# Gate weight sums beside branch B, and the gate products without sums first

## The chip, the cores and the metric

The kernel runs on one core of a Trainium2 chip. The metric is device time in microseconds. The core has five engines with a queue of instructions each: TensorE (PE, matrix products), VectorE (DVE), ScalarE (ACT), GpSimd (POOL) and SyncE (SP), which here issues every DMA. Each queue is worked off in its own order; an instruction that waits for a semaphore holds back all that stand behind it on its queue.

## The reference, cut to what matters

One encoder block: two attention branches, merged by gates, then a feed-forward part. The gates are what the change is about.

```
h = concat([meta, x])                                # 16 + 1024 tokens, width 1024
proj = rms_norm(h, norm_mix) @ w_in                  # qa ka va | qb kb vb | ga gb
y_a = differential_attention(qa, ka, va, ...)        # branch A: 4 heads, two softmaxes each
y_b = windowed_gqa(qb, kb, vb, sink)                 # branch B: 8 heads, a window of 128
merged = sigmoid(ga) * (y_a @ w_ba) + sigmoid(gb) * (y_b @ w_bb)
h = h + merged @ w_o
h = h + (silu(n @ w_ff_gate) * (n @ w_ff_up)) @ w_ff_down      # n = rms_norm(h, norm_ffn)
out = rms_norm(h, norm_final)[:, 16:]
```

## The kernel before, in words

All matrix products run on operands split in a high and a low part (three matmuls: high by high, high by low, low by high). The normalized tokens lie transposed in SBUF as `hT_hi` and `hT_lo`, and the projections (`project`, line 204 issues their matmuls) run over them, one block of 128 columns of `w_in` after another; each block's weights are loaded to `w_c`, split by ACT (`wh_c`) and POOL (`wl_c`), with two buffers each. In the names, c1280 is the block va2, c768 is ka2, c384 is qa3.

The gate projections (`ga`, `gb`: 16 blocks of 128 columns, 1024 tokens) are computed by a scheme of the Strassen kind: for each of eight chunks `k` of 256 columns seven half-size products `p` (numbered 1 to 7) take the place of eight. Products 2 and 1 use plain weights and plain tokens. Product 3 uses a sum of weights with plain tokens, product 4 plain weights with a sum of tokens, products 5, 6 and 7 sums of both. So two sets of sums are made ahead:

- the token sums (`token_sums`, lines 512 to 529, POOL adds, buffers `ta` and `to` in the pool `tpool`), stored to DRAM as `ts_d` beside branch B's first unit, and brought back later over the part of `hT` that is no longer needed (`load_sums`, line 568);
- the weight sums (`weight_sums`, lines 585 to 597): for each chunk two loads `gw`, four POOL adds (lines 592 to 595) and four stores to `ws_d`. They use a pool of their own, `wspool`.

Order of the stages: normalization and the first projections; unit 0 of branch B (`units_b`, eight score tiles of four heads) mixed with the projections of branch A's heads 0 and 1; the projection qb of unit 1, whose stores `qb` place it for the scores; unit 1 mixed with the projections of heads 2 and 3; then branch A, 32 tiles (head `h`, tile `t` of 128 tokens). In branch B a tile's scores (`bps`) go through DVE and ACT to `bs`, POOL scales them (line 330), PE transposes (`bpt`) and multiplies with the values (`bpy`), and the result goes out as `yb_d`. In branch A a tile's two score rows (`aps`, line 745) go through DVE (line 748), ACT's exponential (line 753), POOL's scaling of the first (line 756) and DVE's combination (line 759), and are transposed (`apt`, line 771) and multiplied with the values (`apy`, line 784).

The gate products fill PE in branch A. `gate_steps` (line 718) is a generator: one step is three matmuls, a product is four steps, and `order_g` lists the 56 products. `fill(n)` takes n steps from it: at the head of branch A (`G_FIRST`), at each later head (`G_HEAD`, 10), and at each "g" of `SLOTS` (5 a tile, 24 tiles) and `SLOTS_LAST` (4 a tile, nine rounds). `HOLD` keeps 36 of the 224 steps for the end. Weights come ahead: `g_load` (line 608; plain ones from `w_in`, sums from `ws_d`, to buffers `gr`) and `g_split` (ACT and POOL, line 118, to `gop`).

In this stage PE's order is the order of the code. On the other engines, and for PE before it, a scheduler sets the order of the whole program from its own estimate of times; once set, it is fixed.

Of the kernel before, what the change touches and what calls it, by code (L numbers as in the profile page):

```python
# [19 lines left out]
P = 128  # L20
# [24 lines left out]
GK_BUFS = 3  # L45
GR_BUFS = 6
GO_BUFS = 4
# [3 lines left out]
G_HEAD = 10  # L51
G_FIRST = 4

# [20 lines left out]
def encoder_block(ctx: ExitStack, tc: tile.TileContext, x, meta, norm_mix, w_in, lq1, lk1, lq2, lk2,  # L74
# [7 lines left out]
    def f32(ap):  # L82
        return ap.bitcast(F32)
# [497 lines left out]
    def g_weights(k, kh, c0, cn):  # L581
        at = (C_GB, C_GA)[k // 4] + k % 4 * 256 + c0
        return w_in[kh * 512:kh * 512 + 512, at:at + cn].rearrange("(c p) n -> p c n", p=P)

    def weight_sums(k, p):
        tt = nc.gpsimd.tensor_tensor
        raw = p.tile([P, 2, 4, 256], F32, tag="raw", name=f"gw_{k}", bufs=2)
        for kh in range(2):
            nc.sync.dma_start(raw[:, kh], g_weights(k, kh, 0, 256))
        a11, a21, a12, a22 = (raw[:, i, :, j * P:j * P + P] for i in range(2) for j in range(2))  # L590
        s1, s2, s3, s4 = (p.tile([P, 4, P], F32, tag="sum", name=f"gs{i}_{k}", bufs=6) for i in range(4))
        tt(s1, a21, a22, ALU.add)
        tt(s2, s1, a11, ALU.subtract)
        tt(s4, a12, s2, ALU.subtract)
        tt(s3, a11, a21, ALU.subtract)
        for i, t in ((5, s1), (3, s4), (6, s2), (7, s3)):
            nc.sync.dma_start(ws_d[i, k], t)

# [37 lines left out]
    qb = new_qb(1)  # L636
    project_qb(1, qb)
    units_b(1, qb)
    close_bpool()
# [11 lines left out]

    def load_a(h):
        p = apool
        qs, ks = [None, None], [None, None]
        for m in (1, 0):
            q = qs[m] = p.tile([P, S], F32R, tag=f"q{m}", name=f"aq{h}_{m}")
            k = ks[m] = p.tile([P, 2, L], F32R, tag=f"k{m}", name=f"ak{h}_{m}")
            nc.sync.dma_start(f32(q), qa_d[h][m])
            nc.sync.dma_start(f32(k)[:, 0, :], ka_d[h][m])
            for hl in range(2):  # L660
                nc.sync.dma_start(f32(k)[64 - 64 * hl:128 - 64 * hl, 1, :], ka_d[h][m, 64 * hl:64 * hl + 64, :])
        v = p.tile([P, 2, 9, P], F32R, tag="v", name=f"av{h}")
        nc.gpsimd.memset(f32(v)[:, 0, 8, :], 0.0)
# [4 lines left out]

    ld = load_a(0)
    wspool, close_wspool = pool("wspool")  # L670
    project_a(2)
    for k in range(4):
        weight_sums(k, wspool)
    project_a(3)
    for k in range(4, 8):
        weight_sums(k, wspool)
    for n in range(2):
        g_load(n, wpool.tile([P, DC, P], F32, tag="w", name=f"w_g{n}", bufs=2)[:, 0:4].rearrange("p c n -> p (c n)"))
        g_split(n, wpool.tile([P, DC, P], F32R, tag=("wh", "wl")[n], name=f"w_gop{n}", bufs=W_BUFS)
                .rearrange("p (a c) n -> p a c n", a=2))  # L680
    g_done[:] = [2, 2]
    load_sums(5, 0, 1)
    flush_v()
    close_psum1()
    close_wspool()
    close_tpool()
# [22 lines left out]
    def gate_steps():  # L709
        for n, (p, k) in enumerate(order_g):  # L710
# [5 lines left out]
            for c in range(4):  # L716
# [3 lines left out]
                if c == 3:  # L720
# [6 lines left out]
                    nc.sync.dma_start(g_place(p, k), st)  # L727
                    if k == 7 and p in (2, 5, 3):
                        load_sums({2: 6, 5: 7, 3: 4}[p], *act)
                yield  # L730
# [720 lines left out]
```

## Time and profile before

| | us |
|---|---|
| median of 3 runs | 1525.5 (1518.1 to 1526.4) |
| the profiled execution | 1522.9 |
| its span | 1521.1 |
| PE, DVE, ACT, POOL busy | 1433.7, 888.8, 679.3, 663.1 |
| end of the projections | 306.8 |
| branch A, first gate step to the last tile's transposes | 306.8 to 655.9 |

The profile is of one execution. Its slices show each engine's busy tenths in 40 equal parts of the span (38 us each) and the clock that TensorE was granted. The list of waits names what ended each idle time. Of the timeline each row is start, duration, engine, line and operands, and in brackets the idle time before it. A row "SPq" is the issue of a DMA, not its transfer. In tables by stretch the columns are named in their first line; where one tile is asked for, they are its engine's busy time and count, the granted clock, the DMA share and GB/s of the stretch.

### The profile page before, as it was taken

The page shows a single profiled execution, that of the slowest core. Times are in us where ns is not written, and L with a number is a line of the kernel's source. Part 1 is how long each engine was busy: PE and PEld are TensorE (multiplying, and loading weights), DVE is VectorE, ACT ScalarE, POOL GpSimd, SP SyncE. Part 2 cuts the span into 40 slices and gives each one's busy share as a digit, 9 for nine tenths or more (in the row PEclk, how much of TensorE's full clock was granted, in tenths as well). Part 3 has the DMA queues.
Part 4 walks back from the last instruction along what each step waited for, and adds up shares of the span by engine and source line. Part 5 has one row for each costly group of instructions (what it writes and reads, how often), then busy time and mean ns, then how long its engine had stood idle before and what let it go on. Part 6 is the DMA issues. An engine that isn't in the chain of part 4 may idle for free.

```text
span 1521.1 us, 21195 instructions
## 1 busy us (share of the span) xinstructions
PE 1433.7 (94%) x7279; PEld 1227.9 (81%) x7279; DVE 888.8 (58%) x1610; ACT 679.3 (45%) x1293; POOL 663.1 (44%) x590
## 2 busy tenths in 40 slices
PE   9999999941699999999999999999999999999997
PEld 7998989931699899987878878888888888788886
DVE  7478336501668687944341596655555554778666
ACT  6466346501466555545431454333333333344444
POOL 4599134328444344333562267545445543000344
PEclk9999999965799999999999999999999999999999
DMA  8457443399364857439650253433333333764443
GB/s 235 110 187 229 115 111 91 89 305 362 119 196 173 282 177 231 131 111 311 192 211 21 97 146 125 139 104 104 104 104 104 104 105 104 282 239 125 137 125 139
DMA packets 185339, 242.41 MB, mean 159 GB/s; under 512 B 18752, under 2 KB 108288, under 8 KB 185232
## 3 DMA queue, kind: packets, MB, share of 16 engines
q1 hardware_dynamic: 185232, 241.07, 49.3%
q8 instruction: 57, 0.93, 0.3%
q14 instruction: 50, 0.41, 0.1%
HBM read 157.45 MB, written 77.00 MB: 154 GB/s over the span
## 4 chain that ended last, share of the span: by engine, by line
PE 72%; DMA 8%; POOL 8%; issue 5%; DVE 3%; ACT 2%; SPq 0%; POOLq 0%; DVEq 0%; ACTq 0%
PE pg L1232 25%; PE pd L1326 8%; PE pg L718 7%; PE po L1009 5%; PE ppa L706 4%; PE aps L745 3%; PE pp_qb L204 3%; PE apy L784 3%; POOL oa L118 3%; PE pp_va L204 2%; PE apt L771 2%; DMA gw<-in_w_in_dram 2%; PE pp_qa L204 2%; PE pp_ka L204 2%; DMA ak<-ka_d 1%
## 5 line engine op out<-in xcount | busy, mean ns | idle before, releaser
L118 POOL TENSOR_TENSOR wop<-wf,wop 128x512 fp32r<-128x512 f32 x128 | 173.3, 1358 | 163.7 <-ACT wop L117 151.4
L1232 PE MATMUL pg<-t,wop 128*128 128x512 f32 x1056 | 242.9, 389 | 0.2 <-POOL wop L118 0.2
L1232 PEld LDWEIGHTS pg<-t,wop 128*128 128x128 f32 x1056 | 198.2, 188 | 41.6 <-POOL wop L118 0.6
L1326 PE MATMUL pd<-ob,oa 128*128 128x512 f32 x924 | 210.2, 390 | 1.3 <-DVE ob L118 0.9
L1326 PEld LDWEIGHTS pd<-ob,oa 128*128 128x128 f32 x924 | 173.4, 188 | 38.0 <-DVE ob L118 1.3
L1232 PE MATMUL pg<-b,wop 128*128 128x512 f32 x792 | 184.0, 390 | 2.3 <-DVE c L1241 2.3
L1232 PEld LDWEIGHTS pg<-b,wop 128*128 128x128 f32 x792 | 148.4, 188 | 33.7 <-issue 2.4
L718 PE MATMUL pg<-hT_hi,gop 128*128 128x512 f32 x432 | 162.7, 399 | 9.9 <-ACT gop L117 7.7
L118 POOL TENSOR_TENSOR gop<-gr,gop 128x512 fp32r<-128x512 f32 x54 | 74.5, 1380 | 121.2 <-ACT gop L117 115.3
L118 POOL TENSOR_TENSOR oa<-ra,oa 128x512 fp32r<-128x512 f32 x33 | 44.0, 1335 | 171.3 <-ACT oa L117 169.9
L117 ACT ACTIVATE wop<-wf 128x512 fp32r<-128x512 f32 x128 | 80.3, 632 | 85.0 <-PE pg L1232 49.3
L745 PE MATMUL aps<-ak,aq 128*128 128x392 f32 (+1 forms) x384 | 96.2, 335 | 13.9 <-DMA ak<-ka_d 13.9
L753 ACT ACTIVATE as<-as,amn 128x1040 f32<-128x1040 f32 x64 | 74.4, 1162 | 76.8 <-DVE amn L748 76.6
L718 PEld LDWEIGHTS pg<-hT_hi,gop 128*128 128x128 f32 x432 | 82.3, 190 | 22.8 <-ACT gop L117 8.0
L117 ACT ACTIVATE oa<-ra 128x512 fp32r<-128x512 f32 x77 | 48.7, 632 | 108.2 <-PE pd L1326 53.2
L745 PEld LDWEIGHTS aps<-ak,aq 128*128 128x128 f32 x384 | 72.1, 195 | 29.9 <-issue 13.8
L1009 PE MATMUL po<-woh,mT 128*128 128x512 f32 x384 | 88.0, 390 | 0.0
L771 PE MATMUL apt<-ident,as 128*128 128x128 f32 x288 | 45.3, 279 | 43.7 <-DVE as L759 43.4
L718 PE MATMUL pg<-hT_lo,gop 128*128 128x512 f32 x216 | 86.1, 398 | 0.0
L1009 PEld LDWEIGHTS po<-woh,mT 128*128 128x128 f32 x384 | 71.9, 188 | 14.8
L1067 DVE TENSOR_TENSOR s<-wf,wf 128x512 f32<-128x512 f32 x22 | 18.8, 856 | 106.6 <-DMA wf<-in_w_ff_gate_dram 55.0
L771 PEld LDWEIGHTS apt<-ident,as 128*128 128x128 f32 x288 | 34.3, 145 | 44.5 <-DVE as L759 43.8
(279 smaller groups left out, 3091.0 us busy)
## 6 DMA issues: line engine op xcount, KB each, us to landing
ra<-aop SPq DMA_DIRECT2D x77, 256.0 KB, 2.7
wf<-in_w_ff_gate_dram SPq DMA_DIRECT2D x24, 512.0 KB, 3.7
wf<-in_w_ff_up_dram SPq DMA_DIRECT2D x24, 512.0 KB, 3.6
aop<-as SPq DMA_DIRECT2D x44, 256.0 KB, 2.1
w_c<-in_w_in_dram SPq DMA_DIRECT2D x17, 512.0 KB, 5.0
aop<-c SPq DMA_DIRECT2D x33, 256.0 KB, 2.0
ts_d<-to SPq DMA_DIRECT2D x16, 512.0 KB, 3.8
gw<-in_w_in_dram SPq DMA_DIRECT2D x16, 512.0 KB, 6.9
```

What stands on the lines that cost most here:

```text
L117: nc.scalar.activation(hi, src, AF.Copy)
L118: lo_eng.tensor_tensor(lo, src, f32(hi), ALU.subtract)
L204: nc.tensor.matmul(ps[:, :n], a[:, c, :], b[:, c, at:at + n], start=(c == 0 and i == 0), stop=(c == DC - 1 and i == 2))
L706: nc.tensor.matmul(ps, w[:, a, j, :], src(j, b, tk), start=(j == 0 and n == 0), stop=(j == 3 and n == 2))
L718: nc.tensor.matmul(ps, op[:, a, c], quad(b, *act)[:, c], start=(p in (2, 5, 1) and c == 0 and i == 0), stop=(p in (2, 3, 4) and c == 3 and ...
L745: nc.tensor.matmul(ps[:, :n], qs[m][:, t * P:(t + 1) * P], ks[m][:, vv, k0:k0 + n], start=(vv == 0), stop=(vv == 1))
L753: nc.scalar.activation(s[m][:, 0:L], s[m][:, 0:L], AF.Exp, bias=low, scale=-1.0, accum_out=dn[:, m:m + 1])
L771: nc.tensor.transpose(pt[:kp, j, :], s[:, k * P:k * P + kp], ident)
L784: nc.tensor.matmul(py[:, cols], v[:kp, a, k, :], at_[:kp, k, b, :], start=(k == 0 and j == 0), stop=(k == 8))
L1009: nc.tensor.matmul(ps, mT[:, c, a, t * P:(t + 1) * P], wos[q, c][:, b], start=(c == 0 and n == 0), stop=(c == DC - 1 and n == 2))
L1232: nc.tensor.matmul(ps, op[:, x, c, :], b[:, y, c, :], start=(p in (1, 2, 5) and c == 0 and n == 0), stop=(p in (4, 2, 3) and c == 3 and n ...
L1326: nc.tensor.matmul(ps[u], oa[:, a, u * P:(u + 1) * P], ob[:, b, :], start=(p in (1, 2, 5) and j == 0 and k == 0), stop=(p in (2, 3, 4) and ...
```

## The change

- The weight sums are made between the projection of qb's unit 1 and that unit's tiles, in halves: a chunk's rows in two pieces `c` of 0 and 2, each with two loads of half the size, four adds of 128x256 for 128x512 and four stores of half the size. They use `tpool`'s buffers, two `to` and three `ta` for all, where `wspool` had two and six.
- `order_g` begins with all eight products 2 (0 to 7); then 5 and 3 in turn; the rest is as before. `G_FIRST` is 28 in place of 4, so that seven products run ahead of branch A's first scores.
- The first two products' weights lie in `tpool`'s buffers in place of `wpool`'s; `GR_BUFS` is 5 in place of 6. The token sums are brought back after (5,3), (5,7) and (3,7), and the first of them between the two parts of head 0's loads, which are now called for after the projections.

```diff
-GR_BUFS = 6
+GR_BUFS = 5
...
-G_FIRST = 4
+G_FIRST = 28
...
-    order_g = [(2, k) for k in range(4)]
+    order_g = [(2, k) for k in range(8)]
     for k in range(0, 8, 2):
         order_g += [(p, k + i) for p in (5, 3) for i in range(2)]
-        if k < 4:
-            order_g += [(2, k + 4 + i) for i in range(2)]
...
-    def weight_sums(k, p):
+    def weight_sums(k):
         tt = nc.gpsimd.tensor_tensor
-        raw = p.tile([P, 2, 4, 256], F32, tag="raw", name=f"gw_{k}", bufs=2)
-        for kh in range(2):
-            nc.sync.dma_start(raw[:, kh], g_weights(k, kh, 0, 256))
-        a11, a21, a12, a22 = (raw[:, i, :, j * P:j * P + P] for i in range(2) for j in range(2))
-        s1, s2, s3, s4 = (p.tile([P, 4, P], F32, tag="sum", name=f"gs{i}_{k}", bufs=6) for i in range(4))
...
+        for c in range(0, 4, 2):
+            raw = tpool.tile([P, 2, 2, 256], F32, tag="to", name=f"gw_{k}_{c}", bufs=2)
+            for kh in range(2):
+                nc.sync.dma_start(raw[:, kh], g_weights(k, kh, 0, 256)[:, c:c + 2])
+            a11, a21, a12, a22 = (raw[:, i, :, j * P:j * P + P] for i in range(2) for j in range(2))
+            s1, s2, s3, s4 = (x[:, i] for x in [tpool.tile([P, 2, 2, P], F32, tag="ta", name=f"gs{j}_{k}_{c}", bufs=3)
+                                                for j in range(2)] for i in range(2))
+            tt(s1, a21, a22, ALU.add)
+            tt(s3, a11, a21, ALU.subtract)
+            tt(s2, s1, a11, ALU.subtract)
+            tt(s4, a12, s2, ALU.subtract)
+            for i, t in ((5, s1), (7, s3), (6, s2), (3, s4)):
+                nc.sync.dma_start(ws_d[i, k][:, c:c + 2], t)
...
     project_qb(1, qb)
+    for k in range(8):
+        weight_sums(k)
     units_b(1, qb)
...
-    ld = load_a(0)
-    wspool, close_wspool = pool("wspool")
     project_a(2)
-    for k in range(4):
-        weight_sums(k, wspool)
     project_a(3)
-    for k in range(4, 8):
-        weight_sums(k, wspool)
     for n in range(2):
-        g_load(n, wpool.tile([P, DC, P], F32, tag="w", name=f"w_g{n}", bufs=2)[:, 0:4].rearrange("p c n -> p (c n)"))
...
+        g_load(n, tpool.tile([P, 512], F32, tag="ta", name=f"w_g{n}", bufs=3))
+        g_split(n, tpool.tile([P, 2, 4, P], F32R, tag="to", name=f"w_gop{n}", bufs=2))
     g_done[:] = [2, 2]
-    load_sums(5, 0, 1)
+    ld = load_a(0, lambda: load_sums(5, 0, 1))
```

How the order moves, at four places. SP's queue around the stores of qb for unit 1, before:

```order
L176 DMA w_c1280_3156<-in_w_in_dram 128x8x128
L357 DMA yb_d0_131<-by1_0_7_1622 64x128 x2
L357 DMA yb_d1_132<-by1_0_7_1622 64x128 x2
L292 DMA qb1_2297<-qk_stage_2323 64x512 x4
L292 DMA qb1_2297<-qk_stage_2355 64x512 x4
L176 DMA w_c768_3241<-in_w_in_dram 128x8x128
L292 DMA qb1_2297<-qk_stage_2393 64x512 x4
L292 DMA qb1_2297<-qk_stage_2425 64x512 x4
L176 DMA w_c384_3362<-in_w_in_dram 128x8x128
```

and now, from the last twelve of those stores on (`gw_4_0` is the first half of chunk 4, `ws_d5_3` the store of product 5's sum of chunk 3):

```order
L292 DMA qb1_2297<-qk_stage_2393 64x512 x4
L597 DMA ws_d3_3_106<-gs1_3_0_2520 128x256
L597 DMA ws_d5_3_98<-gs0_3_2_2532 128x256
L597 DMA ws_d7_3_122<-gs1_3_2_2533 128x256
L597 DMA ws_d6_3_114<-gs0_3_2_2532 128x256
L597 DMA ws_d3_3_106<-gs1_3_2_2533 128x256
L292 DMA qb1_2297<-qk_stage_2425 64x512 x4
L588 DMA gw_4_0_2542<-in_w_in_dram 128x2x256 x2
L588 DMA gw_4_2_2555<-in_w_in_dram 128x2x256 x2
L176 DMA w_c1280_3344<-in_w_in_dram 128x8x128
L176 DMA w_c768_3429<-in_w_in_dram 128x8x128
```

The weights of va2 and ka2 moved behind all stores of qb and behind the first ten half-chunks' loads. POOL's queue at the end of the weight sums, before (`as1_0_0` is the first score tile of branch A):

```order
L592 TENSOR_TENSOR gs0_7_3742<-gw_7_3739 128x512
L593 TENSOR_TENSOR gs1_7_3743<-gs0_7_3742,gw_7_3739 128x512
L594 TENSOR_TENSOR gs3_7_3745<-gw_7_3739,gs1_7_3743 128x512
L595 TENSOR_TENSOR gs2_7_3744<-gw_7_3739 128x512
L756 TENSOR_SCALAR as1_0_0_3815<-as1_0_0_3815,adn_0_0_3814,neglam_878 128x1040
```

and now (`bs_1_4` is tile 4 of branch B's unit 1):

```order
L595 TENSOR_TENSOR gs1_7_0_2624<-gw_7_0_2620,gs0_7_0_2623 128x256
L118 TENSOR_TENSOR wl_c1408_3619<-w_c1408_3616,wh_c1408_3618 128x1024
L593 TENSOR_TENSOR gs1_7_2_2637<-gw_7_2_2633 128x256
L595 TENSOR_TENSOR gs1_7_2_2637<-gw_7_2_2633,gs0_7_2_2636 128x256
L330 TENSOR_SCALAR bs_1_4_2909<-bs_1_4_2909,bdn_1_4_2911 128x432 x4
```

The last sum stands ahead of a tile of branch B now, where it stood ahead of a tile of branch A. PE's queue in tile 3_4 of branch A, before:

```order
L745 MATMUL aps_3_4_1_0_6629<-ak3_1_6188,aq3_1_6187 128x392 x2
L718 MATMUL pg1_4_6391<-hT_hi_159,gop6_4_6296 128x512
L718 MATMUL pg1_4_6391<-hT_lo_160,gop6_4_6296 128x512
L718 MATMUL pg1_4_6391<-hT_hi_159,gop6_4_6296 128x512
L745 MATMUL aps_3_4_1_392_6636<-ak3_1_6188,aq3_1_6187 128x392 x2
L718 MATMUL pg1_4_6391<-hT_hi_159,gop6_4_6296 128x512
```

and now:

```order
L742 MATMUL aps_3_4_1_0_6800<-ak3_1_6398,aq3_1_6397 128x392 x2
L742 MATMUL aps_3_4_1_392_6804<-ak3_1_6398,aq3_1_6397 128x392 x2
L742 MATMUL aps_3_4_1_784_6808<-ak3_1_6398,aq3_1_6397 128x256 x2
L781 MATMUL apy_3_1_6780<-at3_0_6465,av3_6409 128x256 x9
L742 MATMUL aps_3_4_0_0_6824<-ak3_0_6404,aq3_0_6403 128x392 x2
```

The gate steps between the scores are gone here, as in all tiles from the third chunk of 3_2 on; they are at the head of branch A. There SP's queue now reads (before, the loads of aq, ak and av came first, then four of gw, then gr):

```order
L608 DMA gr2_2_3858<-in_w_in_dram 128x4x128
L608 DMA gr2_3_3860<-in_w_in_dram 128x4x128
L660 DMA aq0_1_3832<-qa_d0_63 128x1024
L661 DMA ak0_1_3833<-ka_d0_67 128x1040
L663 DMA ak0_1_3833<-ka_d0_67 64x1040 x2
L660 DMA aq0_0_3840<-qa_d0_63 128x1024
L661 DMA ak0_0_3841<-ka_d0_67 128x1040
L663 DMA ak0_0_3841<-ka_d0_67 64x1040 x2
L668 DMA av0_3846<-va_d0_71 128x2x1024
L608 DMA gr2_4_3873<-in_w_in_dram 128x4x128
```

Two products' weights moved ahead of the loads for branch A, the next ones stand behind them.

More of the change, by code (lines that the diff above doesn't have):

```diff
@@ L650, in encoder_block, with load_a @@
         nc.gpsimd.tensor_copy(dist_m[:, t, 0:S - last_k0], dist[:, u0 + last_k0:u0 + S])
-    def load_a(h):
+    def load_a(h, between=lambda: None):
         p = apool
@@ L661, in load_a @@
                 nc.sync.dma_start(f32(k)[64 - 64 * hl:128 - 64 * hl, 1, :], ka_d[h][m, 64 * hl:64 * hl + 64, :])
+            if m:
+                between()
         v = p.tile([P, 2, 9, P], F32R, tag="v", name=f"av{h}")
@@ L727, in gate_steps @@
                     nc.sync.dma_start(g_place(p, k), st)
[L728 to L729 removed]
+                    if (p, k) in ((5, 3), (5, 7), (3, 7)):
+                        later_p = {(5, 3): 6, (5, 7): 7, (3, 7): 4}[p, k]
+                        load_sums(later_p, *G_ACT[later_p])
                 yield
```

9 lines of the change are left out of this document (removed).

## The prediction

> **What bounds the kernel now.** I read the slices of the page first, then the waits of PE over the whole span.
>
> ```profile
> PE   9999999941699999999999999999999999999997
> PEclk9999999965799999999999999999999999999999
> DMA  8457443399364857439650253433333333764443
> ...
> PE apt L771 <- DVE as L759: 43.4, 2, 42.7
> PE aps L745 <- DMA ak<-ka_d: 13.9, 4, 10.5
> PE pg L718 <- ACT gop L117: 7.7, 1, 7.7
> PE pg L718 <- POOL gop L118: 2.2, 1, 2.2
> ```
>
> TensorE is full in every slice but those around 300 to 390 us, and the granted clock drops in the same slices. Nearly all its waiting is at four places of that stretch. The stretches by engine:
>
> ```profile
> core 0: us, PE busy (x) PEld busy (x) DVE busy (x) ACT busy (x) POOL busy (x), PEclk, DMA share, GB/s
> 84.00:150.00 66.00, 65.51 (x390) 60.39 (x388) 53.01 (x96) 41.43 (x94) 60.85 (x55) 1.00 0.64 200
> ...
> 602.04:647.80 45.76, 45.59 (x296) 41.91 (x295) 42.14 (x120) 27.33 (x52) 15.43 (x13) 1.00 0.43 135
> 306.70:389.40 82.70, 19.98 (x68) 15.20 (x66) 6.77 (x25) 8.73 (x15) 46.09 (x38) 0.61 0.96 319
> 150.00:306.00 156.00, 156.00 (x913) 142.25 (x913) 78.97 (x179) 76.76 (x175) 49.36 (x70) 1.00 0.39 106
> ```
>
> The hole, 306.7 to 389.4, is 82.7 us. Its end in order of time:
>
> ```profile
> 333.65 1.26 POOL L592 TENSOR_TENSOR gs<-gw 128x512 f32<-128x512 f32 x1 [37.40 <-DMA gw<-in_w_in_dram]
> ...
> 386.96 1.26 POOL L595 TENSOR_TENSOR gs<-gw 128x512 f32<-128x512 f32 x1
> 388.21 1.20 POOL L756 TENSOR_SCALAR as<-as,adn,neglam 128x1040 f32<-128x1040 f32 x1
> ...
> 389.45 2.29 DVE L759 SCALAR_TENSOR_TENSOR as<-as,adn,as 128x1040 f32<-128x1040 f32 x1 [36.10 <-POOL as L756]
> ```
>
> POOL makes all eight chunks of weight sums first; L756, the first score tile's own step, stands behind them in its queue, DVE behind L756, and PE's transposes behind DVE.
>
> **Term 1, the hole.** It holds this PE work (gate matmuls, then score matmuls):
>
> ```profile
> 306.70:389.40 82.70, 15.23 (x42) 0.61 0.96 319
> 306.70:389.40 82.70, 8.14 (x24) 0.61 0.96 319
> ...
> 597.96 0.40 PE L718 MATMUL pg<-hT_hi,gop 128*128 128x512 f32 x1
> 598.66 0.52 PE L745 MATMUL aps<-ak,aq 128*128 128x392 f32 x2
> 599.02 0.39 PE L718 MATMUL pg<-hT_hi,gop 128*128 128x512 f32 x1
> ```
>
> At the full clock a gate step (three matmuls) takes 598.66 − 597.96 = 0.70 us and a wide score pair 0.36; the narrow pair I estimate by width at 0.24. 14 steps are 9.8, 8 wide and 4 narrow pairs 3.9, together 13.7. So 82.7 − 13.7 = **69.0 us** are lost here. With the sums made before 306 nothing on POOL stands ahead of L756.
>
> **Term 2, what comes late next at this place.** In the changed order PE runs seven products (28 steps × 0.70 = 19.6 us) before the first scores. Two have their weights already (tpool's buffers); the third waits for SP.
>
> ```profile
> 306.78 0.39 PE L718 MATMUL pg<-hT_hi,w_gop 128*128 128x512 f32 x1
> ...
> 311.38 0.61 SPq L658 DMA_DIRECT2D aq<-qa_d  x1
> ...
> L664 SPq DMA_DIRECT2D av<-va_d x1: 569/569/569, 317.3 to 317.3; - x1
> ...
> DMA to landing us min/median/max: 5.8/7.6/13.6
> ```
>
> Count from T, the end of the last projection (306.78 now). Products one and two end at T+5.7. SP issues gr_2 behind the last yb_d stores, at about T+4.7 (the place of aq now: 311.38 − 306.78 = 4.6); its small neighbours land in 3.3 to 4.2 (rows below), ACT's split adds 0.6: product three starts near T+9.7, a gap of 4. Three and four run to T+16. gr_4 is issued behind aq, ak and av, 4.1 MB. Now these are issued from 311.38 and the last piece of av, the longest landing of its rows, is there at 317.3 + 13.6 = 330.9, with two megabytes of hT_hi and gw among them. At the 319 GB/s of the hole's row 4.6 MB take 14.5 us: gr_4 at T+20, product five at T+21.5, a gap of 5. With 1.5 us of cooled clock the seventh ends at T+31.6; minus 19.6, **12 us** stay lost. Least: the first gap alone, 4. Most: av's time as now (T+24) and then a landing of 6 us with the rest behind it, 24. I take 12, nearest to the byte count.
>
> **Term 3, the sums beside branch B.** The adds are 64 of 128x256 instead of 32 of 128x512. They take POOL 64 × 0.68 = 44 us (half of 1.26, plus the slowdown beside a busy DVE, below) where it has 156 − 49 = 107 idle: hidden as work. Their place in the queues is not. SP gets 94 issues between the last token-sum store and the load of hT (32 loads of 256 KB and 62 of the 64 stores of 128 KB; the bytes are those of before): at 0.58 us each (the rows of qb and w_c below), 55 us more.
>
> ```profile
> 180.81 0.56 SPq L176 DMA_DIRECT2D w_c<-in_w_in_dram  x1
> ...
> L292 SPq DMA_DIRECT2D qb<-qk_stage x16: 461/587/1989, 184.2 to 204.9; - x16
> ...
> 213.33 0.34 PE L204 MATMUL pp_va<-hT_hi,wl_c 128*128 128x384 f32 x1
> ...
> L176 SPq DMA_DIRECT2D w_c<-in_w_in_dram x7: 374/554/633, 147.7 to 235.7; - x7
> ...
> DMA to landing us min/median/max: 3.9/4.2/5.7
> ...
> L608 SPq DMA_DIRECT2D w_g<-in_w_in_dram x2: 374/457/540, 258.7 to 282.1; - x2
> ...
> DMA to landing us min/median/max: 3.1/3.3/3.5
> ...
> L117 ACT ACTIVATE wh_c<-w_c x9: 1042/1047/1065, 141.7 to 273.7; 128x1024 fp32r<-128x1024 f32 x9
> ...
> 250.48 2.43 POOL L330 TENSOR_SCALAR bs<-bs,bdn 128x432 f32<-128x432 f32 x4 [6.83 <-DVE bdn L328]
> ```
>
> The load of va2's weights (w_c1280), at 180.81 now, comes to stand behind all 16 qb stores and the loads of half-chunks eight and nine, which wait for the buffers of six and seven. A half takes about p = 7 us: 2.7 of adds, 1.2 of two issues ahead of the store that frees its buffer, 3.1 for that store (taken like w_g's load, a little under). Eight halves from 148 end at 204; with every new row laid behind the old ones one by one I get the issue at 210. Add 4.2 landing, 1.05 for ACT, POOL's rows ahead and 2.4 for the low half: 220.7, where PE needs it at 213.33. That is 7.4 late. A second measure: tile 4's scaling of unit 1 (L330, 250.48 now) is queued on POOL behind the last sum, which ends at 148 + 16p = 260, 9.5 late, and its consumers have some slack. Both delays are the same delay seen twice; I take **8 us**. Least: behind the last qb store (204.9) and five issues the load is out at 207.8, ready at 215.5: 2. Most: the landings of the hole,
>
> ```profile
> gw<-in_w_in_dram SPq DMA_DIRECT2D x16, 512.0 KB, 6.9
> ws_d<-gs SPq DMA_DIRECT2D x32, 256.0 KB, 5.5
> ```
>
> give p near 9 in the same layout and 36 us. The stage's DMA share is 0.39 against 0.96 there, so the low end is nearer.
>
> **Term 4, the end of branch A.** The 188 gate steps of the loop were spread as 4 + 30 + 120 + 36 = 190 slots; with 28 at the head they run out 24 slots early, and the last six tiles (3_2 to 3_7) have none. Nothing of PE's work is gone; DVE now bounds those tiles. The row 602.04:647.80 above is six tiles with four steps each; of its DVE time this is the gate adds:
>
> ```profile
> 602.04:647.80 45.76, 3.36 (x5) 1.00 0.43 135
> ```
>
> Bare, DVE needs 42.14 − 3.36 = 38.8 for six and PE 45.6 − 24 × 0.70 = 28.8. With DVE as full as in that row (92%) they take 42.1; PE idles 42.1 − 28.8 = 13.3: **13 us**. Least 10 (DVE wholly full), most 17 (as long as now).
>
> At nothing: GR_BUFS 5 for 6 (a product lasts several us of slots, a load lands in 4), the later loads of token sums (issued seven to thirteen products ahead of their first use), the first two products' weights, now in tpool, whose last sums are long gone, and the issue of the first token sums ahead of the scores' loads (their room is free once the second of the last three chunks is projected).
>
> **Sum.** −69 + 12 + 8 + 13 = −36. The profiled execution took 1522.9 (span 1521.1), 2.6 under the median of 1525.5 and inside the runs' 1518 to 1526; 1522.9 − 36 = **1487 us**. Under 0.5%, 7.6 us, a difference can't be told from none.
>
> **The rivals.** *Starved queues (0.16), the one on the other side.* SP's order is fixed, so a late POOL add holds qb and w_c back, and these hold PE. With p = 10.5 the last sum ends at 148 + 168 = 316, and L330 of tile 4 starts 66 us late: 1522.9 − 69 + 12 + 66 + 13 = 1545. It decides from p = 9.1 (loss 44: no gain) and 9.5 (slower). Against it: between 84 and 150 POOL is 92% busy with the like token sums and PE still 99%. For it: the 94 new issues are 55 of the 112 us from 148 to 260, on a queue in which old rows wait too.
>
> *Half clock in the bare tiles (0.08).* Their PE is busy 68%. The hole ran at 0.61 granted clock; at that, 28.8 become 47 for six tiles, 5 more than DVE's 42, and at half 58, 16 more: 1503. The Trainium skill (TensorE: Matmul & The Clock Gate, Part 1) has the clock halved after an idle window of some 3.4 us; by that rule this does not happen, since the idle of a bare tile is about 2.2 us and comes in pieces. The rows agree in the hole (7.7 us idle, clock 0.61) and show nothing of shorter gaps.
>
> *Loads first (0.14).* Term 2 at its upper end, 24: 1499.
>
> *POOL locked by DVE (0.06).* Beside a DVE at 80% busy adds of 128x512 took longer than alone in the hole:
>
> ```profile
> L521 POOL TENSOR_TENSOR ta<-hT_lo 128x512 f32<-128x512 f32 x3 | 4.4, 1471 | 0.0
> ...
> L592 POOL TENSOR_TENSOR gs<-gw 128x512 f32<-128x512 f32 x8 | 10.1, 1265 | 46.0 <-DMA gw<-in_w_in_dram 42.7 <-issue 3.2
> ```
>
> That is 1.47 against 1.27, 16%; DVE is half busy beside branch B, so I used 8%, 0.68. If each add waited out a whole DVE operation of about 0.6, p grows by 2.4 to 9.4 and the loss to 48: 1527. The Trainium skill (SBUF — State Buffer, Who interferes with whom) speaks of an exclusive lock held for the whole instruction; the 16% says that few adds meet it.
>
> *Nothing late in branch B (0.12).* Term 3 at 2: 1481.
>
> The forecast, 1478 to 1497, has 0.44. Range 1471 to 1512: below it all least ends together (4 + 2 + 10 gives 1470), above it most of the starved queues and the lock. Faster 0.85 (all but 0.15 of those two), same 0.06, slower 0.09.
>
> **What would show it.** Right: no L592 to L595 after 306; PE with two gaps of 4 to 5 us after the last projection and its first scores about 31 us after T; a wait of some 8 us of PE for wl_c or bs between 205 and 265; no pg in the last six tiles and DVE over 90% there. Wrong: T itself beyond 330 (queues), a clock under 0.9 in the last tiles, or scores later than T+40.

## The result, and the profile after

The changed kernel takes 1498.1 us (median of 4 runs, 1495.5 to 1501.9) against 1523.3 for the kernel before: a ratio of 0.984, with a 95% interval of 0.980 to 0.988. It is faster by 25 us where 36 were forecast; 1498 lies in the range of 1471 to 1512. The profiled execution took 1498.8 us, its span 1496.9.

The slices of the page (PE, its granted clock, the DMA engines), and the longest waits of PE:

```profile
PE   8999989996999999799999999999999999999997
PEclk9999999998999999999999999999999999999999
DMA  8366778549367747048640345333333333864443
```

```profile
PE pg L714 <- ACT gate_stage L722: 12.0, 1, 12.0
PE apt L768 <- DVE as L756: 7.0, 3, 2.6
PE bpt L343 <- POOL bs L330: 5.5, 1, 5.5
PE pp_qb L204 <- DVE qk_stage L223: 3.0, 1, 3.0
...
PE bps L318 <- DMA qb<-qk_stage: 2.0, 2, 1.5
```

The slices with 4, 1 and 6 of before (304 to 418 us) are one slice with a 6 now (337 to 374); new are the 8 of the sixth (187 to 225) and the 7 of the seventeenth (599 to 636); the 8 of the first lies ahead of anything that was changed. The wait of 42.7 us for `as` is gone. In its place stand one of 12.0 at the head of branch A, three of 1.8 to 2.6 in its last tiles, and several of up to 5.5 around qb, 178 to 230 us.

The same by stretches (names of the columns in the first line): beside branch B, at the head of branch A, and its last tiles.

```profile
core 0: us, PE busy (x) PEld busy (x) DVE busy (x) ACT busy (x) POOL busy (x), PEclk, DMA share, GB/s
150.00:200.00 50.00, 47.01 (x264) 42.08 (x263) 16.17 (x35) 18.36 (x37) 29.04 (x37) 0.97 0.72 217
200.00:225.00 25.00, 19.84 (x88) 15.63 (x86) 5.81 (x18) 4.37 (x12) 7.54 (x11) 1.00 0.78 227
225.00:250.00 25.00, 22.23 (x121) 20.53 (x122) 12.05 (x25) 13.84 (x31) 21.59 (x31) 0.86 0.89 264
...
329.40:365.85 36.45, 23.66 (x84) 18.06 (x85) 0.00 (x0) 8.01 (x14) 10.19 (x8) 0.77 0.91 267
596.20:641.20 45.00, 36.78 (x240) 33.12 (x239) 39.45 (x123) 25.69 (x50) 10.63 (x9) 0.92 0.13 48
```

Beside branch B the DMA engines are busy 0.72 to 0.89 from 150 to 250 us, where the kernel before had 0.39 over 150 to 306, and PE loses time in a stretch that was full. The head takes 36.5 us for 28 steps (19.6 at full clock), the last tiles 45.0 us with PE idle for 8.2.

Three rows divide the execution: the first matmul of qb for unit 1, the first gate step (T), and the first matmul of the stage after branch A (`ppa`). They are in the list of one tile's instructions (durations, then first and last start). Before:

```profile
L204 PE MATMUL pp_qb<-hT_hi,wh_c x32: 388/392/398, 176.6 to 199.3; 128*128 128x512 f32 x32
...
L706 PE MATMUL ppa<-yb,wbhb x192: 388/389/793, 691.3 to 737.6; 128*128 128x512 f32 x192
```

After, with T, a row of the timeline, behind:

```profile
L204 PE MATMUL pp_qb<-hT_hi,wh_c x32: 388/395/628, 181.2 to 205.5; 128*128 128x512 f32 x32
...
L702 PE MATMUL ppa<-yb,wbhb x192: 389/389/504, 670.1 to 716.6; 128*128 128x512 f32 x192
```

```profile
329.38 0.80 PE L714 MATMUL pg<-hT_hi,w_gop 128*128 128x512 f32 x1 [1.39 <-DVE by L353]
...
355.47 0.80 PE L714 MATMUL pg<-hT_hi,gop 128*128 128x512 f32 x1 [11.98 <-ACT gate_stage L722]
...
365.85 0.52 PE L742 MATMUL aps<-ak,aq 128*128 128x392 f32 x2
```

| us | before | after | difference |
|---|---|---|---|
| start to qb | 176.6 | 181.2 | +4.6 |
| qb to T (term 3) | 130.2 | 148.2 | +18.0 |
| T to ppa (terms 1, 2, 4) | 384.5 | 340.7 | -43.8 |
| ppa to the end | 829.8 | 826.8 | -3.0 |
| span | 1521.1 | 1496.9 | -24.2 |

Of the first row's 4.6 us, 3.0 are a wait right ahead of qb's first matmul:

```profile
181.15 0.50 PE L204 MATMUL pp_qb<-hT_hi,wh_c 128*128 128x512 f32 x1 [2.99 <-DVE qk_stage L223]
```

A piece of ka was staged late there, because ACT had waited 8.1 us for a store of va, and the stores of sums stand between these stores in SP's queue. The kernel before has no such wait, so the 3.0 us belong to the sums too, though the table leaves them outside term 3. The rest of the row, and most of the last row, is chance: in the profiled executions of the experiments below, which change nothing ahead of the first sum, qb begins between 176.2 and 180.3 (with 0 to 3.3 of this wait), and from `ppa` to the end they take 826.2 to 829.0.

Term 3's stretch holds 11.2 us in which PE is idle and 137.0 in which it is busy, at a granted clock of 0.95; before, it was busy for all 130.2 at 1.00. So of the 18.0 us, 11.2 are waits and 6.8 slower work. The waits are 7.5 in unit 1's first tile (2.0 for qb, 5.5 for its scaling on POOL), 3.2 in branch B's last tile, which the new order puts last before T, and 0.4 for va2's weights.

### The profile page after: what moved, and what is told of

Same layout as the page of the kernel before. It is cut to its first block, busy times and chain, and to the rows that moved or that the text cites. A ratio compares the mean times of both kernels' runs of the same rounds, so it can differ in the third digit from the quotient of the medians.

```text
span 1496.9 us, 21310 instructions
## 1 busy us (share of the span) xinstructions
PE 1439.3 (96%) x7279; PEld 1228.5 (82%) x7279; DVE 885.1 (59%) x1610; ACT 679.0 (45%) x1293; POOL 667.6 (45%) x622
## 4 chain that ended last, share of the span: by engine, by line
PE 75%; DMA 7%; POOL 6%; issue 5%; DVE 3%; SPq 2%; ACT 2%; POOLq 0%; ACTq 0%; DVEq 0%
PE pg L1229 26%; PE pg L714 8%; PE pd L1323 8%; PE po L1006 5%; PE ppa L702 4%; PE aps L742 3%; PE pp_va L204 3%; POOL oa L118 3%; PE apy L781 3%; PE pp_qa L204 2%; PE apt L768 2%; PE pp_ka L204 2%; DMA ak<-ka_d 2%; PE bps L318 1%; PE bpt L343 1%
## 5 line engine op out<-in xcount | busy, mean ns | idle before, releaser
L742 PE MATMUL aps<-ak,aq 128*128 128x392 f32 (+1 forms) x384 | 92.0, 329 | 2.4 <-DVE at L772 0.7
L1064 DVE TENSOR_TENSOR s<-wf,wf 128x512 f32<-128x512 f32 x22 | 25.2, 1145 | 105.9 <-DMA wf<-in_w_ff_gate_dram 58.0
L742 PEld LDWEIGHTS aps<-ak,aq 128*128 128x128 f32 x384 | 68.7, 188 | 17.6 <-DVE amn L745 2.1
L745 DVE CUSTOM_DVE_ANT_0 as<-aps,dist,far_a 128x392 f32<-128x392 f32 x64 | 39.6, 619 | 51.8 <-PE aps L742 51.1
L320 DVE CUSTOM_DVE_ANT_0 bs<-bps,tbx,nsink 128x432 f32<-128x432 f32 (+1 forms) x64 | 38.1, 623 | 50.4 <-PE bps L318 38.2
```

The lines of the kernel that those rows point to most:

```text
L742: nc.tensor.matmul(ps[:, :n], qs[m][:, t * P:(t + 1) * P], ks[m][:, vv, k0:k0 + n], start=(vv == 0), stop=(vv == 1))
L745: nc.vector.tensor_tensor_reduce(s[m][:, k0:k0 + n], ps[:, :n], far_by, slope, low, ALU.add, ALU.min, mn[:, m, i:i + 1])
```

## The experiments

Two columns are read from the profiled executions as in the table above; the ratio is to the kernel before in the same session, whose median lay between 1518.8 and 1521.2.

| run | median us | ratio (95%) | qb to T | T to ppa |
|---|---|---|---|---|
| changed kernel | 1498.1 | 0.984 (0.980 to 0.988) | 148.2 | 340.7 |
| e1, four steps a tile | 1490.3 | 0.980 (0.977 to 0.983) | 147.2 | 332.9 |
| e2, weights first | 1500.7 | 0.986 (0.983 to 0.989) | 147.5 | 341.1 |
| e3, va2's weights early | 1506.0 | 0.990 (0.987 to 0.993) | 145.8 | 349.4 |
| e4, no adds | 1505.4 | 0.988 (0.985 to 0.991) | 147.5 | 354.9 |
| e5, weights first and room | 1496.5 | 0.984 (0.981 to 0.988) | 147.6 | 341.2 |
| e6, two stores a half | 1503.1 | 0.990 (0.987 to 0.993) | 146.7 | 355.7 |
| e7, no stores | 1498.7 | 0.987 (0.985 to 0.989) | 143.6 | 347.0 |
| e8, sums alone | 1489.8 | 0.981 (0.979 to 0.984) | 147.3 | 338.1 |
| e9, qb from ACT | 1502.7 | 0.986 (0.982 to 0.991) | 146.8 | 352.9 |
| e10, head of 16 | 1491.6 | 0.980 (0.977 to 0.984) | 147.5 | 333.6 |
| e11, pause for qb | 1481.3 | 0.973 (0.970 to 0.976) | 141.6 | 333.9 |
| e12, pause and four products | 1484.5 | 0.975 (0.973 to 0.978) | 140.4 | 334.5 |

One side effect must be known for both columns. Whatever changes the work of the sums also changes the scheduler's fixed order. In e3, e4, e6, e7, e9, e11 and e12 PE's last work before T became the projection of ka3, alone or mixed with branch B's last tile, and the 3.2 us of waits in that tile shrank to between 0 and 1.4. So 1.8 to 3.2 us of what these seven runs gain from qb to T is the order's doing. In the first five of them the loads of the third product's weights also went behind those of aq, ak and av. There PE waited 18.8 to 23.2 us for them, in e3

```profile
PE pg L715 <- ACT gop L117: 18.8, 1, 18.8
```

So in these five the total time says nothing of term 3. The column from qb to T does, once the end of the stretch is taken out. In the six runs that keep the changed kernel's order up to T (the changed kernel, e1, e2, e5, e8, e10) it lies between 147.2 and 148.2, and PE's wait for qb between 1.5 and 4.2.

### e1: the bare tiles (term 4)

```diff
-SLOTS = "sgsgsngsgsgstntnt"
+SLOTS = "sgsgsngsgsstntnt"
```

> SLOTS gets four gate steps a tile for five, as SLOTS_LAST has: 28 + 30 + 96 + 36 = 190 slots for 188 steps, so none of the last tiles is bare. Theory (the bare tiles cost 45.0 us for about 34 us of PE work, and tiles with four steps keep PE full, as 45.59 of 45.76 us in the profile of before): the 10 to 11 us come back, 1498 - 10 = 1488 (1485 to 1492). Rival (DVE is the bound of every tile with four steps, only evened out): 24 tiles lose 0.4 us each and the time stays at 1498 (1495 to 1501).

T to ppa fell by 7.8 us, to 332.9; the ratio went from 0.984 to 0.980, and the two intervals overlap, so the times alone do not settle it. The theory holds in the trace, at three quarters of its size: the bare tiles were a loss that a more even spread gives back, and tiles with four steps do not become DVE's.

### e2 and e5: the wait of 12 us at the head (term 2)

e2 issues the weights of products 3 to 7 ahead of the loads of branch A:

```diff
-    ld = load_a(0, lambda: load_sums(5, 0, 1))
...
-    g_ahead(0)
+    g_ahead(3)
+    ld = load_a(0, lambda: load_sums(5, 0, 1))
```

> The weights of products 3 to 7 are issued ahead of the loads of aq, ak and av. Theory (the wait of 12.0 us before product 5 is for one load of 256 KB behind 4.1 MB): that wait is gone, the first scores come at T + 22 to T + 25 in place of T + 36.5, and the time is 1498 - 12 = 1486 (1484 to 1490). Rival (bytes in flight are the bound, whatever the order): the same wait stands before the first scores or the first values, 1496 to 1500.

The wait did not go away (13.1 us at the same place). In ACT's timeline it has another cause now:

```profile
352.04 0.59 ACT L722 COPY gate_stage<-pg 128x512 f32<-128x512 f32 x1 [14.52 <-DMA g_d<-gate_stage]
```

The third product's copy needs one of two buffers, the first of which is free when the store of product 1's result has landed, and that store stands behind aq, ak and av. So e5 adds buffers:

```diff
+                        if 2 <= n < 5:
+                            st = apool2.tile([P, 512], F32, tag="g2", name="gate_stage2", bufs=3)
+                        else:
                             st = gpool.tile([P, 512], F32, tag="g", name="gate_stage", bufs=G_BUFS)
```

> As the run with the weights of products 3 to 7 ahead of aq, ak and av, and with three more buffers for the products' results (products 3 to 5 are staged there). Theory (there the 13.1 us moved to the results: ACT's third copy waited 14.5 us for the store of the first, issued behind av): with room for five results that wait is gone; the eighth product's weights, issued behind av, still hold ACT some 5 us, so the first scores come at T + 25 to T + 29 and the time is 1498 - 9 = 1489 (1484 to 1493). Rival (bytes: the loads of aq, ak and av themselves are what everything waits for): the wait stands before the first scores or values, first scores at T + 33 or later, 1496 to 1502.

Again a wait, of 10.2 us, and again behind the same transfers; ACT:

```profile
355.82 0.63 ACT L117 ACTIVATE gop<-gr 128x512 fp32r<-128x512 f32 x1 [13.94 <-DMA gr<-in_w_in_dram]
```

This is the split of the eighth product's weights, issued behind av; the copy that frees the seventh product's bank stands behind it in ACT's queue. First scores came at T + 36.5 in the changed kernel, T + 37.3 in e2, T + 34.6 in e5. e5's theory had named this wait, at 5 us. So the theory of one load in the wrong place falls, and the rival's times hold: in all three kernels, what is issued behind the 4.1 MB for branch A is late, and each of them issues something behind it that PE needs before the first scores. A head with the eighth product's weights ahead as well was not run.

### e8: the sums alone

```diff
-G_FIRST = 28
+G_FIRST = 4
```

with `order_g` and the places of the later token sums as in the kernel before the change.

> The weight sums beside branch B as in the changed kernel, but the order of products and the 4 steps at the head as before. T is as in the changed kernel. Theory H (the 28 steps at the head buy little, since PE waits there anyway, and cost the bare tiles): PE waits 16 to 18 us for aq and ak after 2.8 us of steps, no tile is bare, 1498 - 10 = 1488 (1484 to 1492). Theory G (without the products PE waits for all of aq, ak and av and a late third product): 25 us or more lost after T, 1497 to 1506.

PE waited for the keys of the first scores at once:

```profile
341.03 0.67 PE L743 MATMUL aps<-ak,aq 128*128 128x392 f32 x1 [9.53 <-DMA ak<-ka_d]
343.47 0.67 PE L743 MATMUL aps<-ak,aq 128*128 128x392 f32 x1 [1.78 <-DMA ak<-ka_d]
350.31 0.41 PE L743 MATMUL aps<-ak,aq 128*128 128x392 f32 x1 [1.84 <-DMA ak<-ka_d]
```

but no tile was bare, and T to ppa is 338.1, 2.6 less than in the changed kernel. Theory H holds. All of the change's gain comes from the moved sums: without the rest the ratio is 0.981 (0.979 to 0.984), with it 0.984 (0.980 to 0.988). The new order of products and the 28 steps at the head gained nothing that these runs can tell: what they filled at the head was missing at the end.

### e10: a shorter head

First scores can come at T + 14 (e8), and 16 steps take 11.2 us.

```diff
-G_FIRST = 28
+G_FIRST = 16
...
-        for what in SLOTS if n < 3 * NT else SLOTS_LAST:
+        for what in SLOTS if n < 10 else SLOTS_LAST:
...
-    ld = load_a(0, lambda: load_sums(5, 0, 1))
...
     g_ahead(0)
+    ld = load_a(0, lambda: (load_sums(5, 0, 1), g_ahead(2)))
```

and e5's buffers (`g_ahead(2)` loads the weights of products 5 and 6 between the two parts of head 0's loads).

> G_FIRST is 16; five gate steps in the first ten tiles and four in the others (188 slots, no bare tile); the weights of products 5 and 6 are issued between the two parts of head 0's loads; three more buffers for results. Theory (four products, 11.2 us, fit into the time that aq and ak of the first scores take, T + 14 in the run with 4 steps at the head; whatever is more only moves steps away from the last tiles): first scores at T + 14 to T + 18, PE loses 5 to 9 us there in place of 16.9 and 2 to 3 in the last tiles in place of 11: 1498 - 17 = 1481 (1477 to 1486). Rival (the total of bytes up to av is the bound, a wait comes at product 5 or at the first values instead): 1487 to 1493, as with 4 steps at the head.

First scores at T + 13.4, as expected; T to ppa 333.6, as in e1 (332.9). The rest of the expected gain was taken by three waits of 1.7 to 3.9 us for copies of results and three of 1.0 to 1.6 for keys; the time, 1491.6, is the rival's.

### e3, e4, e6, e7, e9: what makes T late (term 3)

Each takes away one suspect between qb and T. e3 calls for va2's weights ahead of the sums:

```diff
+    ensure(2)
     for k in range(8):
         weight_sums(k)
```

> The load of va2's weights is called for ahead of the weight sums and goes out before the last qb stores. Theory S (SP's place of this load makes T late): va2 starts some 10 us earlier, T = 329 - 8 = 321 and the time 1490 (1487 to 1493). Theory P (POOL's queue does: the scaling of tiles 3 and 4 stands behind the last sums): T stays at 326 to 331 and the time at 1498 (1495 to 1501).

Counted from qb's first matmul, va2 started 3.9 us earlier (43.8 for 47.7) and T came 2.4 earlier, of which 1.8 are the waits before T. T itself is at 322.0, near theory S's 321, but qb began 5.0 us earlier in this execution. PE's wait for va2's weights was only 0.4 us in the changed kernel, so there was little to win here. e4 drops the adds:

```diff
-            tt(s1, a21, a22, ALU.add)
-            tt(s3, a11, a21, ALU.subtract)
-            tt(s2, s1, a11, ALU.subtract)
-            tt(s4, a12, s2, ALU.subtract)
-            for i, t in ((5, s1), (7, s3), (6, s2), (3, s4)):
+            for i, t in ((5, a11), (7, a21), (6, a12), (3, a22)):
```

> Leaves out the 64 adds of the weight sums: the four quarters of the raw weights are stored in the place of the sums, so the gates are computed from other weights; loads and stores keep their number and bytes. Theory P (POOL's queue makes T late): T = 310 to 314, the time 1482 (1478 to 1487). Theory S (the 96 loads and stores do, on SP and in the DMA engines): T = 322 to 329, the time 1492 to 1499.

POOL is nearly idle around qb (1.13 us of 20, with 5.71 in the changed kernel), and PE loses as much:

```profile
176.00:200.00 24.00, 20.92 (x95) 17.03 (x94) 6.12 (x10) 7.26 (x12) 4.81 (x2) 1.00 0.76 222
200.00:220.00 20.00, 15.27 (x58) 11.99 (x58) 3.79 (x13) 3.68 (x11) 1.13 (x3) 0.83 0.86 230
```

From qb to T still 147.5. POOL's adds alone are not the cause. e6 halves the stores:

```diff
-            for i, t in ((5, s1), (7, s3), (6, s2), (3, s4)):
-                nc.sync.dma_start(ws_d[i, k][:, c:c + 2], t)
+            for j in range(2):
+                nc.sync.dma_start(ws_2[j, k][:, :, c:c + 2], two[j])
```

> The four sums of a half go out in two stores of 256 KB for four of 128 KB: 32 issues fewer on SP, the same bytes, the same adds. From the first matmul of qb for unit 1 to T the kernel before took 130, the changed one 147 to 148 us. Theory I (SP's issues are what is late): 32 x 0.55 = 18 us of SP are gone, this stretch takes 135 to 141, the time 1486 to 1492. Theory B (the bytes in the DMA engines): the stretch stays at 145 to 149, the time 1495 to 1501.

146.7, with a wait of 7.6 us for qb: the number of issues on SP alone is not it. e7 leaves the stores out:

```diff
-            for i, t in ((5, s1), (7, s3), (6, s2), (3, s4)):
-                nc.sync.dma_start(ws_d[i, k][:, c:c + 2], t)
```

> Leaves out the 64 stores of the sums; products 5, 3, 6 and 7 load plain weights in their place, so the gates are other numbers. The adds and the loads stay. If stores (issues or bytes) are what makes T late: the stretch from qb's first matmul to T takes 131 to 137 in place of 147 to 148, the time 1482 to 1488. If the loads or the adds are: 141 to 148, 1492 to 1500.

143.6, 4.6 less, short of the 131 to 137 expected. Without stores the loads run ahead at POOL's pace, so the DMA engines are no emptier when qb comes (0.79 and 0.88 in 176 to 200 and 200 to 220), and PE waited 6.2 us for qb. e9 takes qb's stores out of SP's queue:

```diff
-                    nc.sync.dma_start(f32(qb)[64 * hl:64 * hl + 64, 2 * jj + par, at:at + n],
+                    (nc.scalar if g else nc.sync).dma_start(f32(qb)[64 * hl:64 * hl + 64, 2 * jj + par, at:at + n],
```

> The 16 stores of qb for unit 1 are issued by ACT, so they no longer stand in SP's queue behind stores of sums that wait for their adds. From qb's first matmul to T the changed kernel takes 147 to 148 us and the kernel before 130. Theory Q (SP's fixed order holds qb back, and with it unit 1's first tile and all behind it): PE's waits for qb and for the first bs go, the stretch takes 135 to 141, the time 1486 to 1492. Theory B (the loads and stores of the sums fill the DMA engines, whoever issues): PE still waits 2 us or more for qb, the stretch stays at 145 to 149, the time 1495 to 1501.

```profile
214.23 0.82 PE L318 MATMUL bps<-kb,qb 128*128 128x288 f32 x2 [6.99 <-DMA qb<-qk_stage]
```

The wait for qb got longer, 7.0 for 2.0, and the stretch stayed at 146.8. That does not acquit SP's queue, since ACT now waits with its own work while it issues: the last quarter of qb was staged 37.7 us after qb's first matmul, where the changed kernel had it staged after 27.3. And SP's queue does hold qb back in the changed kernel. That quarter is staged by 208.4, and its stores go out from 215.2 on:

```profile
209.72 2.39 SPq L292 DMA_DIRECT2D qb<-qk_stage  x4
212.20 2.95 SPq L597 DMA_DIRECT2D ws_d<-gs  x5
215.24 3.88 SPq L292 DMA_DIRECT2D qb<-qk_stage  x4
```

Counted from qb's first matmul, the last of its 16 stores was issued after 28.3 us in the kernel before, 37.3 in the changed one and 36.6 to 39.9 in the five runs. The stores then landed in 2.3 us (median) before, 2.7 in the changed kernel and 3.2 to 6.2 in the five. So qb goes out some 9 us late in all of them, and in some its transfers are slower as well. What the five have in common is that loads or stores of sums still stand between qb's stores, or go through beside them.

### e11 and e12: no sums while qb goes through

e11 starts from e10. The sums of chunks 0 to 2 run as before; POOL writes four row minima of unit 1's first tile into the buffers of the next loads, so these wait for that tile:

```diff
     for k in range(3):
         weight_sums(k)
+    first_b = [attend_b(1, 0, qb)]
+    for k in range(3, 8):
+        weight_sums(k, k == 3)
-    units_b(1, qb)
+    units_b(1, qb, first_b)
...
+            if after:
+                nc.gpsimd.tensor_copy(raw[:, 0, 0, 0:4], b_min[0])
```

> As the run with 16 steps at the head, and the sums of chunks 3 to 7 start only when the first scores of unit 1 are there (POOL writes four of their row minima into the buffer of the first load of chunk 3, which that load then overwrites). So loads and stores of sums are out of the way while qb is stored and read back. Theory B (transfers of the sums beside qb's are what makes T late): PE's wait for qb goes under 1 us and the stretch from qb's first matmul to T takes 132 to 138 in place of 147; the time is 1491 - 11 = 1480 (1475 to 1486). Rival (it is the sum of transfers and POOL's queue over the whole of unit 1, wherever they stand): the last sum ends near 300, the scalings of tiles 4 to 6 are late instead, the stretch stays at 143 to 149 and the time at 1488 to 1495.

The time is the one expected, 1481.3, but by half the mechanism: from qb to T 141.6, and PE still waited 3.4 us for qb. On the chip the stores of chunk 2 were not out when qb's came: the last store of qb was issued after 32.2 us, and the median landing was 6.1. e12 therefore pauses after chunk 1, and prepares the weights of products 3 and 4 before T too, in the projections' buffers (the first three results are staged in e5's buffers for that):

```diff
-    for k in range(3):
+    for k in range(2):
         weight_sums(k)
...
+    for n in range(2, 4):
+        g_load(n, wpool.tile([P, DC, P], F32, tag="w", name=f"w_g{n}", bufs=2)[:, 0:4].rearrange("p c n -> p (c n)"))
+        g_split(n, wpool.tile([P, DC, P], F32R, tag=("wh", "wl")[n - 2], name=f"w_gop{n}", bufs=W_BUFS)
+                .rearrange("p (a c) n -> p a c n", a=2))
-    g_done[:] = [2, 2]
+    g_done[:] = [4, 4]
...
-        for what in SLOTS if n < 10 else SLOTS_LAST:
+        for what in "ssssss" if n == 0 else SLOTS if n < 15 else SLOTS_LAST:
```

> As the run with the pause, but the pause begins after chunk 1 in place of chunk 2; the weights of the first four products (16 steps at the head) are all loaded and split before T, in buffers of the projections; tile 0 has no gate steps, tiles 1 to 14 have five, the others four. Theory B (what matters is that no sums are in flight beside qb): PE's wait for qb goes from 3.4 to under 1 us, the stretch from qb's first matmul to T from 141.6 to 133 to 138; the wait of 8.7 us for the third product's weights goes, the first scores come at T + 13 to T + 17, and a wait of up to 6 us for the fifth product's weights comes in tile 1. Time 1481 - 4 - 4 = 1473 (1467 to 1479). Rival (the sums that start later are late at the other end: the last one at 285 to 290 holds the scaling of tiles 4 and 5): stretch 140 to 146, time 1478 to 1485.

```profile
176.00:200.00 24.00, 23.05 (x104) 18.76 (x104) 6.11 (x10) 7.37 (x12) 6.25 (x4) 1.00 0.76 209
200.00:220.00 20.00, 20.00 (x101) 17.41 (x101) 8.29 (x25) 9.66 (x24) 12.00 (x16) 1.00 0.77 215
220.00:240.00 20.00, 20.00 (x128) 19.02 (x127) 12.74 (x31) 11.95 (x30) 14.13 (x22) 1.00 0.76 235
240.00:260.00 20.00, 20.00 (x125) 18.45 (x124) 13.19 (x31) 12.10 (x29) 15.85 (x24) 1.00 0.77 234
280.00:300.00 20.00, 14.85 (x89) 13.71 (x88) 7.18 (x19) 7.80 (x20) 11.96 (x16) 0.89 0.53 152
```

Now PE is full from 200 to 260, where e4 and the changed kernel had lost up to 6 us in 20, with no wait for qb left; va2 starts at 214.7 (before: 213.0). Nothing of the sums stands between qb's stores on SP; the last was issued after 27.0 us, and the median landing was 2.3. That shows what the sums beside qb cost. It is not the DMA share as such: from 176 to 220 that is 0.76 and 0.77 here, with PE idle for 0.95 us, and 0.76 and 0.75 in the changed kernel, with PE idle for 5.0. The trace points to the places in SP's queue; no run takes these away and leaves the transfers. And the stretch is still 140.4, where 3.2 of the 7.8 us gained are the waits before T: the last sum ends at 283.7 and PE loses 5.2 us in 280 to 300, where it waits 4.7 for `btr` of a late tile. The rival of e12 is right too: part of term 3 went, and 10.2 us of it stay with the sums wherever they are. Whether these are POOL's queue or the transfers was not separated.

At the head the wait for the third product's weights was replaced by waits for keys:

```profile
PE aps L757 <- DMA ak<-ka_d: 10.5, 5, 3.0
PE bpt L346 <- DVE btr L350: 5.1, 2, 4.7
```

T to ppa is 334.5, the same as in e1, e10 and e11 with heads of 28, 16 and 16 steps. e11 and e12 are faster than both kernels, by 1.1 and 0.9% of the time before against the changed one; between them there is no difference.

## Why the prediction came out as it did

**Direction and range** were right, and the forecast was 11.8 us under the profiled execution. By the table: term 3 gave +10.0 (18.0 for 8), the time before qb +4.6 and the time after ppa -3.0, neither of which the prediction had, and terms 1, 2 and 4 together +0.2 (-43.8 for -69 + 12 + 13 = -44). That these three came out so close is luck: each was off, and the errors cancel. That the total fell into the range is owed to its width, since term 3 with the 3.0 us before qb is 21.0, where 8 were said.

**Term 1**, 69 us, holds in its mechanism: the last sum is at 274.1, and no add of sums stands ahead of L756. In size it was 2.4 short. The prediction closed the hole at 389.4, where DVE's L759 starts; PE's wait ends when L759 is done:

```profile
391.80 2.18 PE L771 MATMUL apt<-ident,as 128*128 128x128 f32 x9 [42.70 <-DVE as L759]
```

With the hole up to there the loss is 71.4.

**Term 2** was 12 and is 36.5 - 19.6 = 16.9. The first gap of 4 did not come (product 3 waited 0.8 in all), the second was 12.0 and not 5, and the cooled clock took 4.1 (PE was busy for 23.66 us with work of 19.6), where 1.5 were put down without a row. The weights of product 5 were there at T + 24.7 where the byte count said T + 20; and it did not see that results and later weights wait behind the same bytes (e2, e5), so that an earlier load would have moved the wait and not ended it. (By its own steps product four ends at T + 15.3 and the seventh at T + 31.4, where T + 16 and T + 31.6 are written; that does not touch the 12.)

**Term 4** was 13 and is 8.2 of idle time and some 2 of slow clock; 7.8 of it came back in e1. DVE was busy 39.45 of 45.0, 88%, where over 90% was said. So the terms were off by -2.4, +4.9 and -2.8, which leaves 0.5 of the difference open.

**Term 3 is the step that failed**, by its size and by its reason. The prediction took "8 us" from two places, the load of va2's weights in SP's queue and the scaling of tile 4 behind POOL's last sum. Both delays exist: the load was issued at 221.4 (said: 210), and the row reads

```profile
274.14 0.73 POOL L595 TENSOR_TENSOR gs<-gw,gs 128x256 f32<-128x256 f32 x1
274.86 2.43 POOL L330 TENSOR_SCALAR bs<-bs,bdn 128x432 f32<-128x432 f32 x4
```

274.9 where 260 was said and 250.5 was before. But PE waited 0.4 us for va2's weights and not at all for tile 4's scaling: both came much later than said, and cost next to nothing. With the load early (e3) the stretch is 2.4 shorter, without the adds (e4) 0.7. PE waits earlier, before qb, for qb and in unit 1's first tile, and the prediction passed over that qb's own stores and that tile's scaling stand behind rows of sums in the same two queues. It had the mechanism at hand in its rival of starved queues (a late add holds qb back), but took it for a matter of a long p only. Its upper end of 36 is also a slip: p of 9 gives 148 + 144 - 250.5 = 41.5 by its own formula.

The bytes were passed over too. The prediction used the DMA share of 0.39 before the change to choose the low end, "the stage's DMA share is 0.39 against 0.96 there, so the low end is nearer". 32 loads of 256 KB and 64 stores of 128 KB are 16.8 MB; over the 123 us from the first sum to the last that is 136 GB/s on top of the 106 of the row before, and the measured 217 to 264 GB/s at 0.72 to 0.89 is that sum. What landed later for it was little in the changed kernel: qb's stores took 2.7 us for 2.3. The queues carry the rest: POOL's scaling of unit 1's first tile had its inputs at 217.2, but stood behind an add that waited for its load, and SP had issued that load at 219.2, right behind the last stores of qb,

```profile
223.17 0.72 POOL L592 TENSOR_TENSOR gs<-gw 128x256 f32<-128x256 f32 x1 [8.37 <-DMA gw<-in_w_in_dram]
...
226.78 1.47 POOL L330 TENSOR_SCALAR bs<-bs,bdn 128x288 f32<-128x288 f32 x3
```

In e4 PE waited for qb, `btr` and va2's weights instead, in e9 for qb.

**The rivals.** Starved queues had the mechanism (an add that waits for its load holds back branch B, and SP's fixed order holds qb back) but p came out at 7.7 us a half, under its 9.1; T came at 329.4, at the edge of the sign named for it (beyond 330). The half clock in the bare tiles came in part: 0.92 over them. POOL locked by DVE did not come: the adds took 0.72 to 0.76 us throughout, and without them T is the same. Loads first came in part: term 2 is 16.9, nearer to the forecast's 12 than to its 24.

## What to carry to other kernels

When work is moved beside a full stage, look in each queue for what its rows will stand ahead of, and add its bytes to that stage's GB/s: a share of DMA read before the move says nothing about the stretch after it. The share alone does not tell the cost either: at 0.75 to 0.77 PE lost 5.0 of 44 us in the changed kernel and 0.95 in e12. Work moved to the head of a stage to fill a wait is only a gain if the place that it leaves does not run dry; here 28 steps at the head bought nothing that 4 did not. And here a wait behind a block of large transfers was not cured by taking loads ahead of it, since results and the next weights queued behind the same block in turn (e2, e5).

## What the runs showed of the chip

**A short wait cooled TensorE's clock.** In the bare tiles four transposes take 0.63 us after a wait of 1.82, but 1.11 after 2.58, both times:

```profile
605.70 1.11 PE L768 MATMUL apt<-ident,as 128*128 128x128 f32 x4 [2.58 <-DVE as L756]
619.47 0.63 PE L768 MATMUL apt<-ident,as 128*128 128x128 f32 x4 [1.82 <-DVE as L756]
...
633.10 1.11 PE L768 MATMUL apt<-ident,as 128*128 128x128 f32 x4 [2.58 <-DVE as L756]
```

The granted clock over these tiles is 0.92, and 0.61 from 605.7 to 609.7. The Trainium skill (TensorE: Matmul & The Clock Gate, Part 1) has the halving after an idle window of about 3.4 us, so by it these waits would have cost nothing more; the measurement decides. What a wait of 2.6 us cost on top can be estimated from the rows behind the first: three rows of four transposes at 1.11, 1.06 and 1.06 us and nine `apy` at 1.61, where such rows take 0.60 and 1.3 in the tile between, so some 1.7 us.

**Another engine's queue did not make the transfers earlier.** With qb's stores issued by ACT they landed in 4.9 us (median; 2.7 from SP in the changed kernel), at a DMA share of 1.02 in 200 to 220, and ACT's own work waited up to 8.3 us behind the issues. The Trainium skill (DMA: Bandwidth & Descriptors, Issuing engines are not separate DMA queues) says that DMAs run on the same 16 engines whoever starts them; nothing in the run speaks against it.

**One issue can take ten times as long as another.** A store of results took SP 3.65 us to issue at 346.2 in the changed kernel, at a DMA share of 1.04, and 0.32 to 0.33 from 355 to 365, at 0.99. So a full share alone does not make an issue slow; what does was not separated. A row of several issues also holds the waits between them: the eight stores of qb in e11 span 7.98 us, though none of them took over 0.63.
